# Layer 1 of a two-layer decoder: the copy of the turned compression values moves to ScalarE, and the compressed products move behind half a query projection

## The chip, the cores and the metric

The kernel runs on one core of one Trainium2 chip. The metric is the device time of one launch in microseconds. A core has five engines with a queue of their own each: TensorE (PE: matrix products and transposes, results to PSUM), ScalarE (ACT), VectorE (DVE), GpSimd (POOL), and SyncE (SP), which issues the loads of the weights. They wait for each other by semaphores.

## The reference

256 tokens of width 1024, two layers, everything in float32. Layer 0 is stick-breaking attention and a squared-ReLU MLP. Layer 1 is sparse attention with three branches (compressed blocks, selected blocks, sliding window), gated and added, and another such MLP; a last norm ends it. What the change touches is the compressed branch. From the stream after layer 0 come keys and values of 4 groups of 64 columns; 15 overlapping blocks of 32 tokens are each run through a small network:

```
blk = kv[:, :, 0][:, idx]                                  # 15 blocks x 32 tokens
blk = blk + transpose(cmp_pos)                             # learned positions in the block
hid = gelu(einsum('bncgf,cfe->bncge', blk, cmp_w1))        # c = 0 keys, 1 values; e = 256 hidden columns
cmp = einsum('bncge,ced->bncgd', hid, cmp_w2)
k_cmp, v_cmp = cmp[:, :, 0], cmp[:, :, 1]
...
sc    = einsum('bqghd,bngd->bghqn', qg, k_cmp) * scale     # 16 heads, 4 heads to a group
p_cmp = softmax(where(valid_c, sc, NEG))
o_cmp = einsum('bghqn,bngd->bqghd', p_cmp, v_cmp)
```

## The kernel before

Weights arrive as 1 MB tiles (`raw`), are split by ACT into a rounded part (`wh`, L125) and by DVE into the rest (`wl`, L126), in halves, and a product is taken as three matmuls of these parts (L177 to L179). Three tiles of each are in flight, so a split waits until TensorE has left an older tile.

Layer 1's attention is `nsa`. Its order is written out by hand in the list `NSA`, and each entry calls one step. Every TensorE instruction of this stage is kept in that order. The other engines' orders are made when the kernel is compiled, by a planner that goes by the program's order and by estimated times. The steps that matter here:

- `('q', g, half)`, `q_proj`: half of query projection g, 24 matmuls into the PSUM tile `pq`. After the second half ACT evacuates it to `qu` (L722). Each half calls `step()` once, which splits the next half of a weight tile if the tile lies at most two ahead of the one in use. `('w',)` is one such call by itself; the one after `('q', 2, 1)` finds nothing to split.
- `('qr', g)`, `q_rot`: the rotation of `qu` to `qr`: a shuffle and two operations on DVE (L727, L730, L731) and a product on POOL (L728).
- `('ge',)`, `gelu`: the activation of the compression's hidden layer, into `hu`, 60 rows (4 groups x 15 blocks).
- `('ch',)`, `cmp_hid`: four transposes turn `hu` into the PSUM tile `pht`; ACT copies all of it to `hidT` (L768); POOL then copies the half of `hidT` that belongs to the values four times side by side to `hv` (L770), so that the product lands in four bands of rows.
- `('ck',)`, `cmp_kv`: the compressed products: keys `pkc` from `hidT`, copied by DVE to `kcb` (L782), and values `pvc` from `hv`, masked by DVE to `vcb` (L789).
- `('S', p)`, `scores`: scores of head pair p for selected blocks and window, eight matmuls `z`; DVE adds the mask and finds the row bound (L858), ACT takes the exponentials with their sums (L860).
- `('M', p)`, `weights`: the factors `rs` on DVE (L867, L869), then four products on POOL (L874).
- `('T', p, banks)`, `turn`: twelve transposes `ptp` of the weighted exponentials, in three groups of four, each group into a PSUM bank; the first and third are copied by ACT (L891), the second by DVE (L889). Its first group reads the first head of the pair, the second and third also need the second head.
- `('cp', hf)`, `cmp_probs`: the compressed scores `psc` from `kcb` and their softmax; `('ct', hf)` turns them; `('V', p)`, `values`, reads `vcb`; `('o', ...)` is the output projection.

PSUM has eight banks, in two pools of four: `bank` (pool a) and `bank2` (pool z). The letters in the list say from which pool a step takes its banks. The list around the change is

```
('q', 2, 0), ('ch',), ('S', 1), ('M', 1), ('ck',), ('q', 2, 1), ('w',), ('T', 0, 'zaa'), ('S', 2, 'azaz'), ('cp', 0),
('q', 3, 0), ('T', 1), ('qr', 2), ('w',), ('M', 2), ('S', 3, 'azaa'), ('ct', 0), ('q', 3, 1), ('M', 3), ('V', 0), ('S', 4),
```

Of the kernel before, what the change touches and what calls it, by code (L numbers as in the profile page):

```python
# [7 lines left out]
F32 = mybir.dt.float32  # L8
# [6 lines left out]
P = 128  # L15
D = 1024
T = 2
NK = D // P
NH = 16
DH = 64  # L20
NP = NH // 2
NG = 4
NC = 15
# [31 lines left out]
def hybrid_kernel(ctx, tc, x, xcols, eye, gcols, gfin, wqk, wv, wo0, wkv, wq, wg, rot, wo1, w1, w2, cw1, cw2, cpos, gate_b, consts, out):  # L55
    nc = tc.nc

    cp = ctx.enter_context(tc.tile_pool(name="cp", bufs=1))
    wp = ctx.enter_context(tc.tile_pool(name="wp", bufs=3))
    sp = ctx.enter_context(tc.tile_pool(name="sp", bufs=2))  # L60
# [14 lines left out]
    def bank(name, dt=F32):  # L75
        return ps.tile([P, 512], dt, tag="a", name=name, bufs=4)
# [95 lines left out]
    def pe(ins):  # L172
        if strict[0]:
            tc.keep_in_program_order(ins)
# [6 lines left out]
    def mm(o, a, b, first, last):  # L181
        pe(nc.tensor.matmul(o, a, b, start=first, stop=last, skip_group_check=True))  # L182
# [368 lines left out]
    def nsa(xk, pt0, ap):  # L551
# [5 lines left out]
        cw2s = ap.tile([P, 2, 2, DH], F32, name="cw2s")  # L557
# [57 lines left out]
        M = NG * NC  # L615
# [146 lines left out]
        def cmp_hid():  # L762
            hu = live.pop("h")
            pt = bank("pht")
            for j in range(4):
                pe(nc.tensor.transpose(pt[:, j * M:(j + 1) * M], hu[:, j * P:(j + 1) * P], ident[0:M, 0:M]))
            hidT = ap.tile([P, 2, 2, M], F32, name="hidT")
            nc.scalar.copy(hidT.rearrange("p c e m -> p (c e m)"), pt[:, 0:4 * M])  # L768
            hv = sp.tile([P, 2, NG, 4, NC], F32, name="hv", tag="y")
            nc.gpsimd.tensor_copy(hv.rearrange("p e g r n -> p (e g) r n"),  # L770
                                  hidT[:, 1].rearrange("p e (g n) -> p (e g) n", g=NG)[:, :, None, :]
                                  .to_broadcast([P, 2 * NG, 4, NC]))
            live["hid"] = hidT, hv

        def cmp_kv():
            hidT, hv = live.pop("hid")
            pc = bank("pkc")
            for e in range(2):
                mm(pc[:, 0:M], w2d[:, e].rearrange("p a d -> p (a d)"), hidT[:, 0, e, :], e == 0, e == 1)
            for hf in range(2):  # L780
                r = slice(hf * DH, (hf + 1) * DH)
                nc.vector.tensor_copy(kcb[r, :, hf * NC:(hf + 1) * NC], pc[r, 0:M].rearrange("p (g n) -> p g n", g=NG))  # L782
            pvc = bank("pvc")
            for g in range(NG):
                for e in range(2):
                    mm(pvc[0:M, g * DH:(g + 1) * DH], hv[:, e, g].rearrange("p r n -> p (r n)"), cw2s[:, 1, e, :],
                       g == 0 and e == 0, e == 1)
            for g in range(NG):
                nc.vector.tensor_tensor(vcb[0:M, g], pvc[0:M, g * DH:(g + 1) * DH][:, None, :].to_broadcast([M, 4, DH]),  # L789
                                        cst[0:M, C_BLK:C_BLK + 4][:, :, None].to_broadcast([M, 4, DH]), op=OP.mult)  # L790
# [38 lines left out]
        w2d = ap.tile([P, 2, 2, DH], F32, name="w2d")  # L829
# [103 lines left out]
        def tokens_n():  # L933
# [5 lines left out]
        strict[0] = True  # L939
        do = {"kv": kv_proj, "xq": tokens_q, "rt": rot_tables, "gt": gather_tr, "ga": gather, "gp": gate_proj, "gq": gate_turn, "kr": keys_rope,  # L940
              "cw": cw_proj, "kt": keys_tr, "q": q_proj, "qr": q_rot, "ge": gelu, "ch": cmp_hid, "ck": cmp_kv, "S": scores,
              "M": weights, "T": turn, "V": values, "cp": cmp_probs, "ct": cmp_tr, "o": o_proj, "r": residual, "xn": tokens_n,
              "w": step}
# [141 lines left out]
```

## Time and profile before

| what | value |
|---|---|
| median of 3 runs | 631.48 us (630.46 to 631.71) |
| the profiled execution: its time / its span | 629.87 us / 628.0 us |
| mean granted TensorE clock of that execution | 0.991 |
| busy: PE / DVE / ACT / POOL | 614.5 / 414.4 / 343.3 / 53.9 us |
| layer 1's attention | about 300 to 450 us of the span |
| HBM read over the span | 106.48 MB, 171 GB/s |

Times in the profile count from the first instruction of the span. The span is shorter than the execution's time by what lies around it, 1.87 us here. In a row, "out<-in" names the tile written and the tiles read, and L182 is the helper through which all single matmuls go, so a matmul is known by its tiles. A duration in a merged row (x4, x24) is that of the whole stretch. Matmuls overlap: the pace of a run of them is the distance of their starts, not the duration of one.

### The profile page before, as it was taken

The page shows a single profiled execution, that of the slowest core. Times are in us where ns is not written, and L with a number is a line of the kernel's source. Part 1 is how long each engine was busy: PE and PEld are TensorE (multiplying, and loading weights), DVE is VectorE, ACT ScalarE, POOL GpSimd, SP SyncE. Part 2 cuts the span into 40 slices and gives each one's busy share as a digit, 9 for nine tenths or more (in the row PEclk, how much of TensorE's full clock was granted, in tenths as well). Part 3 has the DMA queues.
Part 4 walks back from the last instruction along what each step waited for, and adds up shares of the span by engine and source line. Part 5 has one row for each costly group of instructions (what it writes and reads, how often), then busy time and mean ns, then how long its engine had stood idle before and what let it go on. Part 6 is the DMA issues. An engine that isn't in the chain of part 4 may idle for free.

```text
span 628.0 us, 9044 instructions
## 1 busy us (share of the span) xinstructions
PE 614.5 (98%) x3555; PEld 518.2 (83%) x3555; DVE 414.4 (66%) x666; ACT 343.3 (55%) x587; POOL 53.9 (9%) x76
## 2 busy tenths in 40 slices
PE   9999999999999999999999969999999999999996
PEld 6899987888888888888888858777888888888885
DVE  5588886776665666666773868864686656666555
ACT  6656665474445544444943757774564444444541
POOL 0100000000000000001221164450000000000000
PEclk9999999999999999999999979999999999999998
DMA  8863334536455554553577421203365555545401
GB/s 298 344 259 135 135 135 144 191 135 222 181 202 200 189 203 154 200 193 135 174 269 293 175 69 68 101 8 128 134 208 194 201 201 168 203 170 203 195 0 68
DMA packets 17899, 108.12 MB, mean 172 GB/s; under 512 B 2368, under 2 KB 3264, under 8 KB 5824
## 3 DMA queue, kind: packets, MB, share of 16 engines
q1 hardware_dynamic: 16560, 105.84, 46.9%
q10 hardware_dynamic: 1296, 1.70, 0.8%
q8 instruction: 28, 0.46, 0.3%
q14 instruction: 15, 0.12, 0.1%
HBM read 106.48 MB, written 1.05 MB: 171 GB/s over the span
## 4 chain that ended last, share of the span: by engine, by line
PE 93%; ACT 2%; DVE 2%; issue 1%; POOL 1%; POOLq 0%; DVEq 0%; ACTq 0%
PE pu L182 28%; PE acc L177 11%; PE acc L178 11%; PE acc L179 11%; PE po L182 3%; PE qk L177 3%; PE qk L179 2%; PE qk L178 2%; PE z L182 2%; PE pk L177 2%; PE pk L178 2%; PE pk L179 2%; PE ptp L185 2%; PE pv L177 1%; PE pv L178 1%; PE pv L179 1%
## 5 line engine op out<-in xcount | busy, mean ns | idle before, releaser
L126 DVE TENSOR_TENSOR wl<-raw,wh 128x1024 fp32r<-128x1024 f32 (+1 forms) x190 | 225.2, 1220 | 124.2 <-ACT wh L125 116.1
L125 ACT CAST wh<-raw 128x1024 fp32r<-128x1024 f32 (+1 forms) x190 | 189.6, 1043 | 109.3 <-PE acc L179 50.8
L182 PE MATMUL pu<-xn,wh 128*128 128x512 f32 x512 | 132.1, 392 | 0.0
L182 PEld LDWEIGHTS pu<-xn,wh 128*128 128x128 f32 x512 | 93.7, 188 | 18.0
L177 PE MATMUL acc<-wh,hh 128*128 128x512 f32 (+1 forms) x256 | 100.1, 391 | 0.0
L178 PE MATMUL acc<-wl,hh 128*128 128x512 f32 (+1 forms) x256 | 99.8, 390 | 0.0
L179 PE MATMUL acc<-wh,hl 128*128 128x512 f32 (+1 forms) x256 | 99.0, 389 | 0.0
L182 PE MATMUL pu<-xn,wl 128*128 128x256 f32 x512 | 76.5, 282 | 0.0
L182 PEld LDWEIGHTS pu<-xn,wl 128*128 128x128 f32 x512 | 72.1, 190 | 5.1
L179 PEld LDWEIGHTS acc<-wh,hl 128*128 128x128 f32 x256 | 48.1, 188 | 10.6 <-DVE hl L355 0.6
L177 PEld LDWEIGHTS acc<-wh,hh 128*128 128x128 f32 x256 | 48.2, 188 | 10.1 <-ACT hh L354 0.9
L178 PEld LDWEIGHTS acc<-wl,hh 128*128 128x128 f32 x256 | 48.2, 188 | 8.6
L354 ACT CAST hh<-ms 128x512 fp32r<-128x512 f32 x32 | 19.8, 619 | 63.0 <-DVE ms L350 63.0
L346 ACT COPY mr<-pu 128x256 f32<-128x256 f32 x64 | 23.6, 369 | 28.0 <-PE pu L182 28.0
L177 PE MATMUL qk<-xa,wh 128*128 128x256 f32 x128 | 37.4, 292 | 0.0
L179 PE MATMUL qk<-xa,wl 128*128 128x256 f32 x128 | 36.3, 284 | 0.0
L178 PE MATMUL qk<-xa,wh 128*128 128x256 f32 x128 | 36.2, 283 | 0.0
L355 DVE TENSOR_TENSOR hl<-ms,hh 128x512 fp32r<-128x512 f32 x32 | 22.1, 691 | 19.2 <-ACT hh L354 19.2
L860 ACT ACTIVATE pe<-pe,nm 128x256 f32<-128x256 f32 (+1 forms) x64 | 28.2, 444 | 9.7 <-DVE nm L858 8.6
L874 POOL TENSOR_TENSOR pe<-pe,rs 128x512 f32<-128x512 f32 (+1 forms) x32 | 30.5, 985 | 28.3 <-DVE rs L869 13.3
L347 DVE TENSOR_TENSOR mu<-pu,mr 128x256 f32<-128x256 f32 x64 | 26.6, 418 | 7.5 <-ACT mr L346 7.5
L177 PE MATMUL acc<-wh,oT 128*128 128x512 f32 x64 | 26.2, 409 | 0.0
(187 smaller groups left out, 854.6 us busy)
## 6 DMA issues: line engine op xcount, KB each, us to landing
raw<-in_w SPq DMA_DIRECT2D x64, 1024.0 KB, 4.8
raw<-in_wqk SPq DMA_DIRECT2D x8, 1024.0 KB, 4.9
raw<-in_wo SPq DMA_DIRECT2D x8, 1024.0 KB, 4.8
raw<-in_wkv SPq DMA_DIRECT2D x6, 1024.0 KB, 4.8
raw<-in_wq SPq DMA_DIRECT2D x4, 1024.0 KB, 5.6
wc<-in_cw SPq DMA_DIRECT2D x4, 1024.0 KB, 6.3
raw<-in_wv SPq DMA_DIRECT2D x6, 512.0 KB, 8.2
raw<-in_wv SPq DMA_DIRECT2D x4, 256.0 KB, 4.3
```

The source lines that it names most:

```text
L125: nc.scalar.copy(h[:, r], raws[j][:, r])
L126: nc.vector.tensor_sub(lo[:, r], raws[j][:, r], f32(h[:, r]))
L177: pe(nc.tensor.matmul(o, a[0], b[0], start=first, stop=False, skip_group_check=True))
L178: pe(nc.tensor.matmul(o, a[0], b[1], start=False, stop=False, skip_group_check=True))
L179: pe(nc.tensor.matmul(o, a[1], b[0], start=False, stop=last, skip_group_check=True))
L182: pe(nc.tensor.matmul(o, a, b, start=first, stop=last, skip_group_check=True))
L346: nc.scalar.copy(r[:, q], pu[:, 256:512])
L347: nc.vector.tensor_add(u[:, q], pu[:, 0:256], r[:, q])
L354: nc.scalar.copy(hh, sv)
L355: nc.vector.tensor_sub(hl, sv, f32(hh))
L860: nc.scalar.activation(e, e, AF.Exp, scale=-1.0, bias=nm[:, hd, t, b:b + 1], accum_out=rs[:, hd, t, b:b + 1])
L874: nc.gpsimd.tensor_tensor(sv, sv, rs[:, hd, t, :][:, :, None].to_broadcast([P, 2, n]), op=OP.mult)
```

## The change

In `cmp_hid` ACT copies only the keys' half of `pht` to `hidT`, and a second ACT copy writes `hv` straight from `pht`, reading each group's 15 columns four times; POOL has no part in it. In the list, `('ck',)` stands behind `('q', 2, 1), ('w',)`, and the turn of step 0 takes two banks of pool z and one of pool a in place of one and two. The matmul of `cmp_kv` indexes `hv` in its new shape.

```diff
-    ('q', 2, 0), ('ch',), ('S', 1), ('M', 1), ('ck',), ('q', 2, 1), ('w',), ('T', 0, 'zaa'), ('S', 2, 'azaz'), ('cp', 0),
+    ('q', 2, 0), ('ch',), ('S', 1), ('M', 1), ('q', 2, 1), ('w',), ('ck',), ('T', 0, 'zza'), ('S', 2, 'azaz'), ('cp', 0),
...
-            hidT = ap.tile([P, 2, 2, M], F32, name="hidT")
-            nc.scalar.copy(hidT.rearrange("p c e m -> p (c e m)"), pt[:, 0:4 * M])
-            hv = sp.tile([P, 2, NG, 4, NC], F32, name="hv", tag="y")
-            nc.gpsimd.tensor_copy(hv.rearrange("p e g r n -> p (e g) r n"),
-                                  hidT[:, 1].rearrange("p e (g n) -> p (e g) n", g=NG)[:, :, None, :]
-                                  .to_broadcast([P, 2 * NG, 4, NC]))
+            hidT = ap.tile([P, 2, M], F32, name="hidT")
+            nc.scalar.copy(hidT.rearrange("p e m -> p (e m)"), pt[:, 0:2 * M])
+            hv = sp.tile([P, 2 * NG, 4, NC], F32, name="hv", tag="y")
+            nc.scalar.copy(hv, pt[:, 2 * M:4 * M].rearrange("p (g n) -> p g n", n=NC)[:, :, None, :]
+                           .to_broadcast([P, 2 * NG, 4, NC]))
...
-                mm(pc[:, 0:M], w2d[:, e].rearrange("p a d -> p (a d)"), hidT[:, 0, e, :], e == 0, e == 1)
+                mm(pc[:, 0:M], w2d[:, e].rearrange("p a d -> p (a d)"), hidT[:, e, :], e == 0, e == 1)
...
-                    mm(pvc[0:M, g * DH:(g + 1) * DH], hv[:, e, g].rearrange("p r n -> p (r n)"), cw2s[:, 1, e, :],
+                    mm(pvc[0:M, g * DH:(g + 1) * DH], hv[:, e * NG + g].rearrange("p r n -> p (r n)"), cw2s[:, 1, e, :],
```

## The prediction

> **What bounds the kernel now.** I read the page first, for the share of each engine; then what TensorE waited for inside layer 1; then each engine's timeline around the one long wait; last the following 30 us, to see whether time won there can be given back.
>
> The page's first part, and TensorE's waits between 300 and 470 us (who waited for whom, total us, times, longest):
>
> ```profile
> PE 614.5 (98%) x3555; PEld 518.2 (83%) x3555; DVE 414.4 (66%) x666; ACT 343.3 (55%) x587; POOL 53.9 (9%) x76
> ...
> PE pvc L182 <- POOL hv L770: 4.4, 1, 4.4
> PE pkc L182 <- ACT hidT L768: 1.1, 1, 1.1
> PE ptp L185 <- DVE nm L858: 0.7, 1, 0.7
> ```
>
> TensorE is the bound: 98% busy, and in this stage three waits in all. Two of them belong to the step that the change moves. The windows give the same place by its clock (column PEclk):
>
> ```profile
> core 0: us, PE busy (x) PEld busy (x) DVE busy (x) ACT busy (x) POOL busy (x), PEclk, DMA share, GB/s
> 360.00:370.00 10.00, 4.55 (x33) 3.55 (x32) 7.70 (x27) 6.16 (x26) 5.20 (x5) 0.73 0.32 107
> ```
>
> The timelines (start, duration, what; in brackets the idle time before it and its releaser). TensorE, from the first half of query projection 2 to the wait for the fourth pair's scores:
>
> ```profile
> 356.65 0.39 PE L177 MATMUL pq<-xq,wh 128*128 128x256 f32 x1
> 359.51 0.28 PE L179 MATMUL pq<-xq,wl 128*128 128x256 f32 x1
> 360.01 1.51 PE L182 MATMUL z<-kT,qr 64*128 64x512 f32 x7
> 362.60 0.66 PE L182 MATMUL pkc<-hidT,w2d 128*128 128x60 f32 x4 [1.08 <-ACT hidT L768]
> 367.63 1.96 PE L182 MATMUL pvc<-cw2s,hv 128*60 128x64 f32 x16 [4.38 <-POOL hv L770]
> 369.52 0.58 PE L177 MATMUL pq<-xq,wh 128*128 128x256 f32 x1
> 371.53 0.28 PE L177 MATMUL pq<-xq,wh 128*128 128x256 f32 x1
> 373.33 1.47 PE L185 MATMUL ptp<-ident,pe 128*128 128x128 f32 x12
> 374.73 1.56 PE L182 MATMUL z<-kT,qr 64*128 64x512 f32 x8
> 376.22 1.97 PE L182 MATMUL psc<-kcb,qu 128*128 128x30 f32 x16
> 378.12 0.36 PE L177 MATMUL pq<-xq,wh 128*128 128x256 f32 x1
> 381.08 1.47 PE L185 MATMUL ptp<-ident,pe 128*128 128x128 f32 x12
> 394.12 1.06 PE L185 MATMUL ptp<-ident,pe 128*128 128x128 f32 x8 [0.66 <-DVE nm L858]
> ```
>
> POOL, which makes hv today, and the end of its weighting step 0:
>
> ```profile
> 362.37 4.66 POOL L874 TENSOR_TENSOR pe<-pe,rs 128x512 f32<-128x512 f32 x4 [3.14 <-ACT wh L125]
> 365.86 1.18 POOL L874 TENSOR_TENSOR pe<-pe,rs 128x256 f32<-128x256 f32 x2
> 366.98 0.59 POOL L770 COPY hv<-hidT 128x480 f32<-128x480 f32 x1
> 371.32 3.19 POOL L874 TENSOR_TENSOR pe<-pe,rs 128x512 f32<-128x512 f32 x4 [3.75 <-DVE rs L869]
> ```
>
> hv's input lies ready at 362.55, but POOL's queue holds the four products of weighting step 0 until 367.04; the copy itself is 0.59 us. TensorE keeps its written order, so the second half of projection 2, whose operands are all there, stands behind pvc.
>
> ACT and DVE in the same stretch:
>
> ```profile
> 361.26 1.03 ACT L125 CAST wh<-raw 128x1024 fp32r<-128x1024 f32 x1
> 362.20 0.35 ACT L768 COPY hidT<-pht 128x240 f32<-128x240 f32 x1
> 365.37 0.51 ACT L860 ACTIVATE pe<-pe,nm 128x256 f32<-128x256 f32 x1 [2.83 <-DVE nm L858]
> 368.80 0.18 ACT L860 ACTIVATION_READ_ACCUMULATOR pe<-pe,nm 128x1 f32 x1
> 373.41 1.05 ACT L125 CAST wh<-raw 128x1024 fp32r<-128x1024 f32 x1 [4.42 <-PE pq L178]
> 374.36 0.59 ACT L722 ACTIVATE qu<-pq 128x512 f32<-128x512 f32 x1
> ...
> 349.84 0.68 DVE L731 TENSOR_TENSOR qr<-qr,qx 128x512 f32<-128x512 f32 x1
> 363.46 1.53 DVE L731 TENSOR_TENSOR qr<-qr,qx 128x512 f32<-128x512 f32 x1
> 367.14 0.44 DVE L782 COPY kcb<-pkc 64x60 f32<-64x60 f32 x2
> 369.62 1.08 DVE L789 TENSOR_TENSOR vcb<-pvc,cst 60x256 f32<-60x256 f32 x3 [2.04 <-PE pvc L182]
> 371.03 0.15 DVE L869 TENSOR_TENSOR rs<-rs,gates 128x8 f32<-128x8 f32 x1
> 374.40 0.69 DVE L889 COPY pT<-ptp 128x512 f32<-128x512 f32 x1 [3.22 <-PE ptp L185]
> 388.24 0.20 DVE L867 RECIPROCAL rs<-rs 128x8 f32<-128x8 f32 x1 [1.87 <-ACT pe L860]
> 393.21 0.41 DVE L858 CUSTOM_DVE_ANT_0 pe<-z,nmask 128x256 f32<-128x256 f32 x1
> ```
>
> The reader is to see ACT idle for 2.83 us just when the new hv copy would run, and DVE and ACT idle again behind pvc: the whole chain had stopped for it. DVE's rows also show that an engine's order is not the program's: rs of step 1, earlier in the program, runs behind vcb.
>
> **The change part by part.**
>
> *The copy hv moves from POOL to ACT.* POOL loses 0.59 us. ACT's one copy of 240 columns (0.35) becomes one of 120 and one of 480. Between 240 columns at 0.35 and 512 at 0.59 (row L722) a column costs 0.24/272 = 0.9 ns: 0.25 us and 0.56 us, 0.46 more than now. The repeated read of each column has no such row in this stretch; as a lower bound I take 0.56, as an upper one 0.69, the mean of the group in which ACT also writes PSUM columns repeatedly (its row is below); I take 0.6, being nearest in length. Behind hidT it then ends about 362.4 + 0.6 = 363.0, inside the idle 2.83. Were that cover gone, it would push the exponentials of step 1 by 0.6.
>
> ```profile
> L597 ACT ACTIVATE kd<-pk,r 128x512 f32<-128x512 f32 x4 | 2.8, 689 | 4.8 <-PE pk L179 4.8
> ```
>
> *The compressed products stand behind the second half of projection 2.* TensorE ends the scores of step 1 at 361.5. The half is 24 matmuls; the first half's went from 356.65 to 359.51, 23 steps, 0.124 each. So it runs 361.5 to 364.4 on warm clock and hides the copies (hv ready at 363.0). Then pkc, 0.66 at most, then pvc: between 1.96 (as it ran) and half of that, 0.98, if all of it was the slowed clock. Products end between 366.0 and 367.0. What goes from TensorE's timeline is the two waits, 1.08 + 4.38 = 5.46, and the slow restart: nine matmuls took 369.52 to 371.53, 2.01 against 9 x 0.124 = 1.12, so 0.89.
>
> [...]
>
> *What is late next: the turn of step 0.* Its twelve transposes read POOL's products. The first four need the third product, about 365.86 + 1.18/2 = 366.45; the others the fourth, 367.04. TensorE arrives between 366.0 and 367.0, so it waits up to 0.45, then up to 0.5. Twelve transposes take 374.73 - 373.33 = 1.40, eight 0.93: the turn ends at 368.05 to 368.4. The scores of step 2 started at 374.73 before; they start 6.3 to 6.7 us earlier.
>
> *Banks.* The turn now takes two banks of the z pool and one of a. Step 1's scores hold all four z banks until VectorE has read them (last read before 367.14), in order, so the first two are free by the turn. In the a pool the products leave pkc and pvc unread a while: kcb at 367.14, then vcb. With only one a bank asked, pht's is free. I cost this at nothing; without that switch the turn would wait for the evacuation of projection 2, which now falls near 365 anyway.
>
> *Queues that the moved step passes.* It issues no DMA and no weight split; the free splitting step that it passes finds nothing to split there, since the second half of the first output weight is split within projection 2's second half, as today (wh at 361.26). On DVE, kcb and vcb (1.44 us) now find their inputs when step 1's reads end, before rs of step 1 wants DVE. ACT's evacuation of projection 2 (0.59, at 374.36 before) comes at 364.4, and the cast that waited for the projection's end (373.41, 1.05) may follow it, ahead of the exponentials of step 1: 0 to 0.6 us late.
>
> *The turn of step 1.* Between the scores of step 2 and it lie the scores, the compressed scores and half of projection 3: 381.08 - 374.73 = 6.35. TensorE would be there at 374.4 to 374.75. It needs POOL's step 1: exponentials end at 369.0 to 369.6, rs a few tenths later, products 3.19 (as step 1 ran) to 4.66 (as step 0 ran, beside DVE work): 372.6 to 375.0. The fourth product is wanted about 374.9. So 0 to 0.5 us of new wait, and the stage is 5.8 to 6.7 ahead there.
>
> *Behind it* the chain by way of exponentials, casts and DVE (to the 0.66 wait at 394.12) hangs on these steps and moves with them, except for work that must be squeezed in: 0 to 0.5. After 394.12 TensorE shows no wait until the last layer's end, so what is won stays.
>
> **Sum:** 6.3 to 6.7 at the scores of step 2, less about 0.25 at the next turn, less about 0.25 of squeezing: 6.0 us. The profiled execution took 629.87 us (span 628.0), which would be 623.9; it lies 1.61 below the median of the runs, 631.48, so against that: 625.5. The forecast's own spread is a gain of 4.9 to 7.4.
>
> **The rivals.**
>
> *Crowding.* DVE had 2.04 + 3.22 + 1.87 = 7.13 us of larger gaps from 367 to its reads of step 4 at 393.21; taking 6.0 out leaves hardly any, and POOL and DVE then work side by side. What that costs the trace shows: step 0's products took 4.66 beside DVE's L731 at 1.53, step 1's 3.19 alone, and L731 0.68 alone. If step 1's products take 1.47 more and rotation 2's sum 0.85 more, both before a turn that waits: 6.0 - 2.3 = 3.7 gained, 627.8. For it speaks that DVE has so little room; against it that most of that work is not wanted at once. [...]
>
> *The wait comes back in ACT's queue, no gain.* If hv's copy stands behind the exponentials of step 1, it ends at 369.0 + 0.6 = 369.6. Then pvc 369.65 to 371.6 on slowed clock, the turn at half speed 2.8, scores of step 2 at 374.4: 0.3 gained, 631.2. Against: the copy is ready by 362.3, three us before the first exponential. Nothing but another order on ACT would do it.
>
> *Slower.* The same place, further back: if the copy also stands behind the two casts that projection 2's end releases (1.05 each), hv ends at 371.7, step 2's scores start at 376.5, 1.8 later than before: 633.3. Zero is where hv ends at about 370.0, slower by more than 0.2% where it ends after 371.3.
>
> **How the numbers follow.** Forecast 0.62; more than 7.4 gained 0.02; crowding (1.3 to 4.9 gained) 0.22; no gain 0.09; slower 0.05. The time is the forecast's, 625.5. The range reaches from 623.3, where every bound falls well, the 0.66 wait goes too and the run lies low, to 628.6, which takes in crowding down to 2.9 gained: 0.62 + 0.02 + 0.17 = 0.81. About 0.2% (1.26 us) is what a measurement of this kernel can tell from no change; so faster 0.86, same 0.09, slower 0.05.
>
> **What would show it.** Right: hv on ACT near 362.5 to 363; the half of projection 2 from 361.5 at 0.12 us a matmul throughout, with a clock of 1.00 in every window; pkc and pvc without a long wait; the turn of step 0 waiting on POOL for under 1 us near 366.5; the scores of step 2 near 368.2; the kernel's last layer about 6 us earlier. Wrong: hv behind L860 on ACT; a new wait over 1 us at a turn (POOL, or DVE's reads of z); a bank wait at the scores of steps 2 or 3; DVE gaps that stay although TensorE waits.

## The result, and the profile after

| | before | after |
|---|---|---|
| median (range), six runs each | 631.07 us (630.38 to 631.71) | 626.02 us (624.84 to 627.69) |
| the profiled execution: time / span / clock | 629.87 / 628.0 / 0.991 | 625.33 / 623.6 / 0.998 |

The ratio is 0.9924 (95% interval 0.9905 to 0.9943): faster by 0.8%, 5.05 us by the medians. The forecast of 625.5 lies 0.5 us below the median. It was reckoned from 631.48, the median of three runs, which is 0.41 above the median of six; the gain itself was forecast at 6.0 us and came out at 5.05.

The page's busy line, and TensorE's waits between 300 and 470 us (who waited for whom, total us, times, longest):

```profile
PE 613.7 (98%) x3555; PEld 516.6 (83%) x3555; DVE 415.8 (67%) x666; ACT 343.9 (55%) x588; POOL 52.1 (8%) x75
```

```profile
PE psc L182 <- ACT pT L890: 0.7, 1, 0.7
PE ptp L185 <- POOL pe L873: 0.5, 1, 0.5
PE pct L185 <- DVE ce L815: 0.5, 1, 0.5
PE z L182 <- ACT qu L722: 0.4, 1, 0.4
PE po L182 <- ACT pcT L824: 0.3, 1, 0.3
```

All three waits of before (4.4, 1.1, 0.7) are gone. Five short ones stand in their place, 2.45 us together; one of them, for POOL, was forecast. The window that showed a clock of 0.73 before:

```profile
360.00:370.00 10.00, 9.07 (x75) 7.08 (x73) 8.72 (x29) 7.52 (x31) 4.67 (x4) 1.00 0.34 106
```

TensorE's timeline (start, duration, what; in brackets the idle time before it and its releaser):

```profile
360.50 1.51 PE L182 MATMUL z<-kT,qr 64*128 64x512 f32 x7
361.94 0.39 PE L177 MATMUL pq<-xq,wh 128*128 128x256 f32 x1
364.79 0.28 PE L179 MATMUL pq<-xq,wl 128*128 128x256 f32 x1
364.90 0.55 PE L182 MATMUL pkc<-hidT,w2d 128*128 128x60 f32 x4
365.38 1.10 PE L182 MATMUL pvc<-cw2s,hv 128*60 128x64 f32 x16
367.02 1.53 PE L185 MATMUL ptp<-ident,pe 128*128 128x128 f32 x12 [0.53 <-POOL pe L873]
368.48 1.13 PE L182 MATMUL z<-kT,qr 64*128 64x512 f32 x4
370.02 0.70 PE L182 MATMUL z<-kT,qr 64*128 64x256 f32 x4 [0.41 <-ACT qu L722]
371.44 1.97 PE L182 MATMUL psc<-kcb,qu 128*128 128x30 f32 x16 [0.71 <-ACT pT L890]
373.33 0.36 PE L177 MATMUL pq<-xq,wh 128*128 128x256 f32 x1
376.29 1.47 PE L185 MATMUL ptp<-ident,pe 128*128 128x128 f32 x12
379.82 0.62 PE L185 MATMUL pct<-ident,ce 128*60 128x128 f32 x4 [0.53 <-DVE ce L815]
385.02 0.65 PE L182 MATMUL po<-pcT,vcb 128*64 128x256 f32 x4 [0.27 <-ACT pcT L824]
```

The half projection runs from 361.94 at 0.12 us a matmul, the products follow without a wait, and the first turn waits 0.53 us. What is new lies behind it. ACT's rows say why; POOL's and DVE's are needed further down:

```profile
362.70 0.24 ACT L768 COPY hidT<-pht 128x120 f32<-128x120 f32 x1
362.84 0.55 ACT L770 COPY hv<-pht 128x480 f32<-128x480 f32 x1
365.87 0.51 ACT L859 ACTIVATE pe<-pe,nm 128x256 f32<-128x256 f32 x1 [2.48 <-DVE nm L857]
...
369.40 0.57 ACT L722 ACTIVATE qu<-pq 128x512 f32<-128x512 f32 x1
369.87 1.03 ACT L125 CAST wh<-raw 128x1024 fp32r<-128x1024 f32 x1
370.81 1.06 ACT L890 COPY pT<-ptp 128x512 f32<-128x512 f32 x2
```

```profile
362.87 4.67 POOL L873 TENSOR_TENSOR pe<-pe,rs 128x512 f32<-128x512 f32 x4 [3.15 <-ACT wh L125]
371.28 3.18 POOL L873 TENSOR_TENSOR pe<-pe,rs 128x512 f32<-128x512 f32 x4
```

```profile
369.52 0.20 DVE L866 RECIPROCAL rs<-rs 128x8 f32<-128x8 f32 x1 [0.99 <-ACT pe L859]
370.67 0.67 DVE L888 COPY pT<-ptp 128x512 f32<-128x512 f32 x1
...
379.68 0.68 DVE L731 TENSOR_TENSOR qr<-qr,qx 128x512 f32<-128x512 f32 x1
```

The evacuation `qu` had its input at about 365, with ACT idle until 365.87, and still ran at 369.40: it stands behind the exponentials of step 1 in ACT's order. It holds a bank that the second half of step 2's scores wants (0.41). Behind it stand a cast and the two `pT` copies, and the compressed scores `psc` want the bank of the first of them (0.71).

Distances from the first scores of step 1 on TensorE, so that what ran ahead of the change drops out (that start is 359.89 before and 360.39 after; the code ahead of it is the same), in us:

| profiled execution | scores of step 2 | half of projection 3 | turn of step 1 | first matmul of the MLP |
|---|---|---|---|---|
| before | 14.84 | 18.23 | 21.19 | 83.44 |
| after | 8.09 | 12.94 | 15.90 | 78.43 |
| the same kernel again | 8.10 | 12.95 | 17.39 | 79.39 |
| ACT copy alone (second time) | 9.79 | 13.18 | 16.13 | 78.68 |
| whole change, `psc` in pool a (second time) | 8.09 | 12.37 | 15.32 | 77.86 |

The last column is called the end of the stage below. The gain is 6.75 us at the scores of step 2, 5.29 at the turn of step 1, and 5.01 at the end of the stage.

### The profile page after: what moved, and what is told of

Read it like the earlier page. It is cut to its first block, busy times and chain, and to the rows that moved or that the text cites. A ratio compares the mean times of both kernels' runs of the same rounds, so it can differ in the third digit from the quotient of the medians.

```text
span 623.6 us, 9045 instructions
## 1 busy us (share of the span) xinstructions
PE 613.7 (98%) x3555; PEld 516.6 (83%) x3555; DVE 415.8 (67%) x666; ACT 343.9 (55%) x588; POOL 52.1 (8%) x75
## 4 chain that ended last, share of the span: by engine, by line
PE 90%; DVE 4%; ACT 3%; issue 1%; DMA 1%; SPq 0%; POOLq 0%; POOL 0%; DVEq 0%; ACTq 0%
PE pu L182 29%; PE acc L177 12%; PE acc L178 11%; PE acc L179 11%; PE po L182 3%; PE qk L177 3%; PE qk L179 2%; PE qk L178 2%; PE z L182 2%; PE pk L177 2%; PE pk L179 2%; PE pk L178 2%; ACT pe L859 2%; PE ptp L185 1%; PE ph L182 1%
```

## The experiments

The median gain is about 1 us short of the forecast's 6.0. Three theories were set up for that part. A: new in-order waits on ACT and DVE, the same in every execution. B: crowding of POOL and VectorE. C: in the stretch of light array work TensorE loses its clock in some executions. B had little left before the first run: POOL's step 1 took 3.18 us after, 3.19 before.

**1. The parts by themselves.** Order and banks of the change, with `hv` still a POOL copy (the five copy and matmul lines as before):

> The new order and banks, with the copy of hv still on POOL. Theory A (what the forecast missed, about 1.2 us, are short waits on ACT's queue after step 0's turn; the long wait itself was POOL's): TensorE reaches pvc at 365.4 and waits for hv until about 368.1 (POOL's step 0 ends at 367.5, copy 0.6): a wait of 2.7 us, short enough for the clock to stay up; step 0's turn starts about 2.2 later than in the changed kernel, but then the waits on qu (0.41) and pT (0.71) find their work done and vanish: 1.0 to 1.3 us slower than the changed kernel, about 627.2, some 3.8 faster than before. Theory B (crowding of DVE and POOL takes the missing time): those waits have nothing to do with it and 2.2 are lost in full: about 628.2, 2.8 faster than before. If the order alone did the work: 626.

Measured: 627.67 us (626.75 to 628.94), ratio 0.9951 [0.9939, 0.9962]. TensorE, and the windows (column PEclk is third from the right):

```profile
368.63 1.96 PE L182 MATMUL pvc<-cw2s,hv 128*60 128x64 f32 x16 [2.67 <-POOL hv L770]
370.52 2.82 PE L185 MATMUL ptp<-ident,pe 128*128 128x128 f32 x12
```

```profile
366.00:368.00 2.00, 0.00 (x0) 0.00 (x0) 2.00 (x15) 1.62 (x7) 2.00 (x4) 1.00 0.79 319
368.00:370.00 2.00, 1.37 (x13) 1.38 (x14) 0.57 (x5) 2.00 (x11) 0.57 (x2) 0.50 0.48 184
...
374.00:376.00 2.00, 2.00 (x13) 1.01 (x9) 0.81 (x5) 1.25 (x2) 1.11 (x2) 0.79 0.00 0
```

The order alone shortens the wait from 4.38 to 2.67 us, and the clock is still halved from 368.0 to 374.8. The time lies between the 627.2 of theory A and the 628.2 of theory B and does not part them, since both had the clock stay up. That a wait of 2.7 us is short enough for that was the author's assumption: no run shows it, and here the clock fell to 0.50 2.1 us into the wait of 2.67, and stayed there for 6.8. Now the ACT copy alone:

```diff
-  ('q', 2, 1), ('w',), ('ck',), ('T', 0, 'zza'),
+  ('ck',), ('q', 2, 1), ('w',), ('T', 0, 'zaa'),      # as before the change
```

> The ACT copy alone; order and banks as before the change. TensorE waits about 1.0 us for hidT at pkc, none for hv; clock up throughout; second half of projection 2 ends near 367.6, so the turn finds POOL's products done (no wait of 0.53). Theory A: scores of step 2 wait for a bank (pvc's, read by vcb near 370.0, then pq's, by qu near 371), 1 to 1.5 us in all, but the compressed scores find a free bank: 0.2 to 0.6 slower than the changed kernel, about 626.4, 4.5 faster than before: nearly all of the gain is the copy's. Rival (the order is what hides the copies): the wait of 1.1 comes back in full on top: 627.2 or more, 3.7 faster than before.

> The ACT copy alone, once more (old order, old banks). Theory C: 625.0 to 626.4 us with clocks of .996 to .998, below the whole change run beside it in its mean clock or equal to it, since its two waits of about 1 us stand between stretches of dense matmuls. Theory A: its waits sum to 3.1 us against 1.9 of the whole change, so it should be about 1 us slower than the whole change: 627.

Measured: 625.61 us (624.99 to 626.42), ratio 0.9919 [0.9906, 0.9932], and again 625.58 (625.13 to 626.58), 0.9915 [0.9901, 0.993]. TensorE, second time:

```profile
363.10 0.66 PE L182 MATMUL pkc<-hidT,w2d 128*128 128x60 f32 x4 [1.00 <-ACT hidT L768]
363.68 1.10 PE L182 MATMUL pvc<-cw2s,hv 128*60 128x64 f32 x16
367.70 1.47 PE L185 MATMUL ptp<-ident,pe 128*128 128x128 f32 x12
370.26 1.56 PE L182 MATMUL z<-kT,qr 64*128 64x512 f32 x8 [1.09 <-DVE rs L868]
```

Two waits of 1.0 and 1.1 us, which the whole change does not have, and yet the same gain. The table says how: its step 2 scores are 1.70 us later than in the whole change, its half of projection 3 only 0.24 later, since the whole change pays 0.41 + 0.71 there and the ACT copy alone does not. The moved list entry wins time that the next bank gives back. Theory A expected 626.4 for the first run; for the second it added up the waits of each kernel and expected 627, and missed: a wait ahead of a later one that would have been paid anyway costs little. And the third part, the bank letters with the old place:

```diff
-  ('q', 2, 1), ('w',), ('ck',), ('T', 0, 'zza'),
+  ('ck',), ('q', 2, 1), ('w',), ('T', 0, 'zza'),
```

> ACT copy with the compressed products at their old place, but the score bank of step 2 changed as in the whole change. Theory A: the 1.10 us wait at step 2's scores for DVE's rs shrinks to 0.3 to 0.6 and a wait of about 0.7 for pT stands at psc instead; 625.2 to 625.8 us. Theory C: the time follows the granted clock and not the waits: with a clock of .996 to .998 it is 625 to 626, and any execution at .993 or less is at 626.5 or more, whatever the waits.

Measured: 625.77 us (625.21 to 626.53), ratio 0.9918 [0.9905, 0.9931]. The 1.09 us wait is gone and none stands at `psc`; short ones appear later (0.33 for `pT` at step 3, 0.52 for `ce`), and the stage takes 78.67. The banks alone are worth nothing, as the order alone on top of the copy is worth nothing that shows.

**2. The wait at `psc`.** The whole change, with a bank of pool a for the compressed scores:

```diff
-  ('T', 0, 'zza'), ('S', 2, 'azaz'), ('cp', 0),
+  ('T', 0, 'zza'), ('S', 2, 'azaz'), ('cp', 0, 'a'),
```

> The changed kernel with the compressed scores of half 0 in a bank of pool a instead of z; the engines' orders stay the same. Theory A: their wait for ACT's copy of pT (0.71 us at 371.44) goes down to under 0.1, since pvc's bank is free at 370.75, and the stage ends 0.4 to 0.7 earlier: about 625.4. Theory B (crowding): TensorE comes to step 1's turn earlier and waits there, or at the turn of the compressed scores, for POOL or DVE as much longer: no change at the output projection, 626.0.

> The whole change with the bank of the compressed products fixed as well, once more: the 0.71 us wait at psc is 0.17. Theory A: 0.5 us under the whole change, 625.5. Theory C: between 624.4 and 626.7, each execution by its clock, median 625.4 to 626.4: no difference that can be measured from the whole change.

Measured: 625.42 us (624.36 to 626.62), ratio 0.9914 [0.9901, 0.9927], and again 624.82 (624.47 to 626.65), 0.9907 [0.9892, 0.9922]. TensorE, second time:

```profile
370.62 1.94 PE L182 MATMUL psc<-kcb,qu 128*128 128x30 f32 x16 [0.17 <-PE z L182]
...
372.48 0.36 PE L177 MATMUL pq<-xq,wh 128*128 128x256 f32 x1
```

The wait is 0.17 in place of 0.71, and the stage 77.86 in place of 78.43: 0.57 us for 0.54 of wait, as theory A says. The first time, with the same waits up to `psc` and the same orders, the stage took 78.84: the clock was halved for 3.4 us. Its row and a window of the fall:

```profile
371.02 1.94 PE L182 MATMUL psc<-kcb,qu 128*128 128x30 f32 x16 [0.17 <-PE z L182]
```

```profile
374.00:376.00 2.00, 2.00 (x12) 2.00 (x11) 2.00 (x5) 2.00 (x11) 1.61 (x2) 0.50 0.00 0
```

**3. The whole change again.** Nothing edited.

> The changed kernel once more, for its spread. Theory C (the array's clock falls to half for one or more stretches of about 3.4 us in some executions, after a stretch with little array work, and that is what the forecast missed): executions split by their mean granted clock: about 0.998 near 625.3, about 0.995 near 626.4, about 0.991 near 627.6; the kernel before shows 0.991 to 0.992 in every one. Theory A (short waits on ACT's queue, the same in each execution): one cluster near 626.0, and the time does not go with the clock.

Measured: 626.49 us (625.68 to 627.8), ratio 0.9932 [0.9919, 0.9944]; clocks 0.991 to 0.996.

```profile
371.58 1.97 PE L182 MATMUL psc<-kcb,qu 128*128 128x30 f32 x16 [0.71 <-ACT pT L890]
```

```profile
374.00:376.00 2.00, 2.00 (x13) 2.00 (x12) 2.00 (x5) 2.00 (x11) 0.60 (x2) 0.59 0.00 0
376.00:378.00 2.00, 2.00 (x12) 2.00 (x12) 2.00 (x4) 1.04 (x5) 0.00 (x0) 0.56 0.00 0
```

Up to `psc` this is the first profile, with the same 0.53 to 0.71 us waits; then the clock is halved for 3.4 us (the two windows of 2 us are short of the full clock by 0.41 and 0.44, which makes 1.70 us lost, and so 3.4 us at half). The half of projection 3 takes 4.44 instead of 2.96 us, the turn of step 1 comes 1.49 later, and by the end of the stage 0.96 is left, as the later 0.53 wait falls away. The executions of this kernel sort roughly by clock: at 0.998 624.84, 625.33, 625.58; at 0.993 to 0.996 five between 625.68 and 626.65; at 0.991 627.49, 627.69, 627.80. The mean clock also counts the program's last microseconds, which run at half clock in every profile (0.50 from 624.01 to 628.0 before, from 621.24 to 623.6 after), so it is no exact count of falls: at 0.996 one profile has a fall inside the stage (`psc` in pool a, the first time) and one has none (the ACT copy alone, the first time). Theory C is shown for its fact: executions of one kernel lose the clock or keep it. The next runs looked for its cause.

**4. Taking the wait at the scores of step 2 away.** `qu` ahead of the exponentials of step 1 on ACT: the scores are split into matmuls and exponentials, and the latter stand behind the projection.

```diff
-  ('S', 1), ('M', 1), ('q', 2, 1), ('w',), ('ck',),
+  ('S', 1, 'zzzz', True), ('q', 2, 1), ('E', 1, True), ('M', 1), ('w',), ('ck',),
```

> The changed kernel with ACT made to evacuate projection 2 (qu) ahead of the exponentials of step 1, as the prediction had it; TensorE's order is the same, one cast then stands ahead of qu and one goes behind step 1's turn copies. Theory A: qu ends near 366.5 instead of 369.97, the wait of 0.41 at the scores of step 2 goes, the copies of step 0's turn come at 370.1 instead of 370.81, compressed scores start near 370.8 instead of 371.44: 0.5 to 0.8 earlier at step 1's turn, about 625.4. Theory B (crowding): exponentials of step 1 end 0.6 later, POOL's step 1 too, and step 1's turn waits: no gain, 626.0 or slower.

Measured: 630.25 us (627.58 to 632.12), ratio 0.9989 [0.9975, 1.0002]. The gain is gone. DVE and TensorE:

```profile
368.30 1.76 DVE L126 TENSOR_TENSOR wl<-raw,wh 128x1024 fp32r<-128x1024 f32 x1
370.08 1.41 DVE L788 TENSOR_TENSOR vcb<-pvc,cst 60x256 f32<-60x256 f32 x4
371.41 0.67 DVE L896 COPY pT<-ptp 128x512 f32<-128x512 f32 x1
```

```profile
372.14 2.60 PE L182 MATMUL psc<-kcb,qu 128*128 128x30 f32 x16 [1.90 <-DVE pT L896]
```

Step 2's scores run without a wait, but with `qu` early the cast and then DVE's weight split come early too, ahead of `vcb` and `pT`; `psc` waits 1.90 for `pT`, and the clock is halved from 373.3 to 380.1 and once more from 397.2 to 400.6. This profile is the slowest of the twelve executions; two with a mean clock of 0.999 took 627.81 and 628.93, so the order costs some 2 to 4 us against the whole change without a fall, and the rest goes with the clock. With the casts of that weight tile pinned behind:

> ACT evacuates projection 2 ahead of the exponentials of step 1, and both casts of the second output weight stand behind the compressed exponentials, so that no split pushes ahead of vcb and pT on DVE. Theory A with the split as the culprit of the slow run of the variant without this: the scores of step 2 do not wait; the compressed scores wait for DVE's copy of pT until about 370.9 (0.9 us) instead of 1.9; stage 0.3 to 0.8 ahead of the changed kernel: 625.3. Theory C: whatever the queues, an execution with a wait of 0.9 just ahead of the compressed scores loses the clock in most executions: mean clock 0.991 to 0.995, 626.5 to 628.

Measured: 626.83 us (624.99 to 627.02), ratio 0.9925 [0.9912, 0.9939]: the gain is back and nothing more; `psc` still waits 0.91 for DVE's `pT`. Its profile has a fall too, from 372.7 to 376.1; the one execution at 0.998 took 624.99.

**5. Dense work in the light stretch.** A half of projection 3 between the scores of step 2 and the compressed scores:

```diff
-  ('S', 2, 'azaz'), ('cp', 0), ('q', 3, 0), ('T', 1),
+  ('S', 2, 'azaz'), ('q', 3, 0), ('cp', 0), ('T', 1),
```

> The changed kernel with the first half of query projection 3 (24 full matmuls) between the scores of step 2 and the compressed scores, instead of behind these. Theory C: the 3.4 us with the least array work (scores, two waits, compressed scores of 30 columns) are broken up, so the clock stays up in every execution: mean clock 0.997 to 0.999. Theory A: the wait for pT (0.71) goes, since pT is copied long before the compressed scores come. Both: 624.6 to 625.2, and by C with a spread under 1 us. If DVE's later start on the compressed softmax holds up its turn, 0.5 to 1.5 come back as a longer wait for ce there: 625.5.

Measured: 628.6 us (628.18 to 629.33), ratio 0.9964 [0.9952, 0.9977]. The `psc` wait is gone, and a longer one comes:

```profile
382.91 1.03 PE L185 MATMUL pct<-ident,ce 128*60 128x128 f32 x4 [3.07 <-DVE ce L815]
```

The compressed softmax starts 3 us later and its chain on DVE now stands on the path. At the end of that wait, at 382.9, the clock fell for 3.4 us. So instead matmuls on zeros: two ahead of the first turn and two ahead of step 2's scores, and then also at the next two turns.

```diff
+            if p == 2:
+                for _ in range(2):
+                    mm(z1[0].rearrange("p b k -> p (b k)"), zero[:, 0:P], zero, True, True)
...
+                if p == 0 and i == 0:        # second kernel: p in (0, 2, 3)
+                    for _ in range(2):
+                        mm(pt, zero[:, 0:P], zero, True, True)
```

> The changed kernel with four idle matmuls of zeros (128x512, about 0.22 us each) on TensorE, two where it waits for POOL ahead of step 0's turn (0.53), two ahead of the scores of step 2, whose later waits (0.41 and 0.71) would take them up; the result is unchanged. DVE's order shifts a little (one split ahead of the reads of step 2), which costs 0.3 to 0.8 at step 1's turn. Theory C: more array work in the light stretch, so no execution falls in clock: mean clock 0.997 or more in all, time 625.3 to 626.0 with a spread under 1 us. Theory A: four more matmuls and the later split cost 0.3 to 0.8 and change no clock: 626.3 to 626.8, spread as before.

> Changed kernel plus two matmuls on zeros ahead of each of four points: the first transposes, the scores of step 2, and the same points of the next two steps (T2, T3). If light array work is what loses the clock in some executions (theory C), filling it at more places raises the mean granted clock to .997 or more in nearly all executions and the time to 625.3 to 626.2 us. If the shortfall is the new in-order waits on ACT and DVE themselves (theory A: the same in every execution), the time stays at 625.7 to 626.8 with the clocks as mixed as before. If each pair of extra matmuls costs its own 0.3 us and buys nothing, 626.5 to 627.5.

Measured: 626.73 us (625.26 to 627.43), ratio 0.993 [0.9918, 0.9943], clocks 0.994 to 0.998; and 627.35 (626.52 to 628.46), 0.9944 [0.993, 0.9958], clocks 0.991 to 0.998. In the first the profiled clock fell at 392.8, behind the compressed scores of the second half of the tokens. The second:

```profile
371.55 2.41 PE L182 MATMUL psc<-kcb,qu 128*128 128x30 f32 x16 [0.71 <-ACT pT L896]
```

```profile
374.00:376.00 2.00, 2.00 (x12) 2.00 (x11) 2.00 (x12) 2.00 (x10) 1.63 (x3) 0.50 0.00 0
```

Both missed what theory C expected: executions lost the clock as before. With four places the median is 0.9 us above the whole change run again (626.49), but the intervals of the two overlap (0.993 to 0.9958 and 0.9919 to 0.9944).

## Why the prediction was right, and where it was off

**The mechanism held.** `hv` ran on ACT from 362.84 for 0.55 us (forecast: until 363.0, for 0.6 us, between 0.56 and 0.69; the stage began 0.50 later), inside the idle time that is now 2.48 in place of 2.83. The half projection began at 361.94 and ran at 0.12 us a matmul. The products ended at 366.5, which less that 0.50 is the early end of the forecast's 366.0 to 367.0; `pvc` took 1.10 where it had taken 1.96 at half clock (0.50 from 366 to 370 us before). The turn waited 0.53 for POOL (forecast up to 0.45, then up to 0.5). The scores of step 2 came 6.75 us earlier, counted from step 1 (forecast 6.3 to 6.7; the early end of the turn was put at 368.05, while the terms given, 367.04 for the fourth product and 0.93 for eight transposes, make 367.97).

**The term of the sum that was mis-sized: what lies between there and the turn of step 1.** It had 0.25. The measured loss is 6.75 - 5.29 = 1.46: waits of 0.41 and 0.71, and 0.34 because the scores of step 2 now run in two pieces with a wait behind each. Their rows last 1.13 + 0.70 = 1.83; before, the next step started 1.49 after them, since the end of one run of matmuls overlaps the start of the next. The 0.71 is the step "Banks. I cost this at nothing": true of the turn's banks, but not of the one that `psc` takes next, which is the turn's first; the run with `psc` in pool a got 0.57 us back. The 0.41 is the sentence that ACT's evacuation "comes at 364.4": it came at 369.40, behind exponentials that became ready after it. The prediction had shown on DVE that an engine's order is not the program's, and did not apply that to ACT. The wait of 0 to 0.5 at the turn of step 1 itself did not come: POOL was done at 374.46, TensorE there at 376.29. Of the prediction's own signs of being wrong one came in small, a bank wait at the scores of step 2 (the 0.41).

**Squeezing** had 0.25: 5.29 - 5.01 = 0.28. The 0.66 wait is gone, waits of 0.53 and 0.27 are new, which makes 0.14 of it; the other 0.14 no row names.

So the stage gained 5.01 us in a profile without a lost clock in the stage, in place of 6.0. What ran ahead of the change gave 0.50 back between these two profiles, as that start moves by up to 1.4 us from run to run; hence 4.54 between the two profiled executions, and 5.05 between the medians. That the time came within 0.5 us of 625.5 is in part luck: the starting value of 631.48 was 0.41 high, and the gain 0.95 short.

**"With a clock of 1.00 in every window"** held for the first profile and failed for the second of the same kernel: a halved clock for 3.4 us, 0.96 us by the end of the stage. The sum counts each remaining wait at its own length alone, as if the clock stayed up through it. No run shows that as a rule: with the order alone the clock fell to 0.50 2.1 us into a wait of 2.67 us, and stayed there for 6.8.

**The rivals.** Crowding (627.8) did not come: POOL's step 1 took 3.18 us, the figure of no crowding, and L731 of rotation 2 its 0.68. In the ACT copy alone POOL's step 1 did take longer, 4.16 us in the second profile, from 370.34 to 374.50; it still ended before TensorE wanted it at 376.60. That DVE's work beside it makes POOL slower was the author's reading of 4.66 us against 3.19; no run took that work away to show it. DVE's order is the next limit, though, as `qu` early (a 1.76 us split ahead of `pT`, 630.25) and the early half projection (a 3.07 us wait for `ce`) show. `hv` behind the exponentials on ACT (631.2) did not come; just this happened to `qu`, where it costs 0.41. The half speed counted there, a turn of 2.8 us, is what the order alone ran at: 2.82 us at a clock of 0.50.

**The parts.** The ACT copy alone gives the whole gain, 0.9919 and 0.9915 against 0.9924 and 0.9932; order alone gives 0.9951. They take away the same wait, so their gains do not add. The version with `psc` in pool a has the lowest ratios of all, 0.9914 and 0.9907; its interval overlaps that of the ACT copy alone (0.9901 to 0.993, on the same chip), so that it is better than that one is not shown.

## What to carry to other kernels

After moving one late operand, follow each PSUM bank one user further than the step that was moved: the next taker of a bank that is now released late is where the time goes back. Ask of every operation that becomes ready early whether its engine's order lets it run early; here one evacuation waited 4 us behind exponentials although its engine was idle when it became ready, and forcing it forward let other work run ahead of what TensorE wanted. When one edit removes the wait, price the other edits in the same change on top of it: here they were worth nothing that shows.

## What the runs showed of the hardware

In these runs the clock did not go by the length of a wait alone. Before, it was halved 1.3 us into the idle time (`pkc` ends at 363.26; this window of before has 0.65, so 1.4 of its 2 us at half):

```profile
364.00:366.00 2.00, 0.00 (x0) 0.00 (x0) 2.00 (x8) 0.63 (x3) 2.00 (x3) 0.65 0.74 172
```

With the order alone it fell 2.1 us into a wait of 2.67 (365.95 to 368.0). In the second run of the changed kernel no wait was over 0.71 us, and it fell at 374.3, in the middle of dense matmuls, 0.9 us behind a stretch of light ones; the ACT copy alone (second time) waited 1.00 and 1.09 us and read 1.00 through the stage. Falls inside the stage lasted 3.4 us or 6.8 us (before; order alone; the first with `qu` early), at a clock of 0.50. The same kernel with the same orders and waits had one in one execution and none in another.

In these profiles the falls stand on a grid. Every profile ends with a fall, behind the last matmuls of the program. Nine profiles have falls inside the stage, ten in all, and each of these lies 228.69 to 259.41 us ahead of the last one, a whole number of steps of 3.413 us (starts read from the clock in windows of 0.1 us):

| profile | falls inside the stage | last fall | steps between |
|---|---|---|---|
| before | 364.60 | 624.01 | 76 |
| order alone | 368.01 | 624.01 | 75 |
| the changed kernel again | 374.34 | 620.10 | 72 |
| `psc` in pool a (first time) | 372.97 | 622.14 | 73 |
| `qu` early | 373.29, 397.18 | 625.88 | 74, 67 |
| `qu` early, cast late | 372.72 | 621.89 | 73 |
| half projection first | 382.88 | 625.23 | 71 |
| zeros at two places | 392.77 | 621.46 | 67 |
| zeros at four places | 372.90 | 622.07 | 73 |

So the clock changed at points 3.413 us apart, and a fall inside the stage lasted one or two steps. The grid is not tied to the program: in the fourteen profiles TensorE comes up to its full pace between 4.0 and 7.1 us of the span. Before, matmuls of 512 columns start 0.43 us or more apart up to 6.0 and 0.23 apart from 6.3; after, up to 6.6 and from 7.0. The grid has a point there in both, 6.20 and 6.84, 181 and 180 steps ahead of the last falls at 624.01 and 621.24 (the clock column reads 1.00 on both sides of it). Which work lies between two of these points therefore changes from execution to execution, although the kernel is the same: `psc` starts 0.63 us ahead of a point (372.07) in the first profile of the changed kernel and 0.65 behind one (370.93) in the second. Before, the step of the grid that ended at 364.60 held the wait of 1.08 us as well as the first 1.3 of the long one.

Why the clock fell at one of these points and not at another stays open. Three of the ten falls came in a wait (before; order alone; half projection first). The other seven began while the sixteen `psc` matmuls of 30 columns ran or up to 0.9 us behind them, and the profiles of the ACT copy alone, which has a dense half projection between `pvc` and the turn, have none in the stage. The author's guess from that is long light stretches; it is not shown, since no run took the `psc` matmuls away. The columns that the matmuls started in a step of the grid move give no sharp line: the ten steps that ended in a fall had 0 to 2512 of them, six others in the stage had as few (from 1896) and kept the clock, and a step of dense projection has about 7000. The first profile of the changed kernel kept it through a step with 2228, its second lost it after one with 2512. The two kernels with zeros settle nothing about them, since none of their added matmuls lay in the step that ended with the fall: with four places the last ones ahead of it ended at 369.1, and that step ran from 369.5 to 372.9; with two, all had ended by 369.1 and it ran from 389.4 to 392.8. At the start of the program, which begins with nine matmuls on zeros, the full pace came, in the profile of the half projection first, while only these had run: they started 0.43 us apart up to 4.0 us, 182 steps ahead of its last fall, and 0.22 apart from there.
